# Spreading the residual gates with rounded products: two rounded parts of each row in place of one plain fp32 row

## The chip, the cores and the metric

The kernel runs on one core of one Trainium2 chip. The metric is the device time of one execution in microseconds (us), the median of the runs shown; a lower time is better.

## What is computed

Four trunk layers update 512 latent tokens (and 256 context tokens) of 1024 channels. Layers 0 and 3 mix the tokens by latent attention, layer 1 by banded attention, layer 2 by long convolutions. What matters here is the frame around the mixers:

```python
for layer in range(4):
    mx = silu(c) @ w_mod[layer] + b_mod[layer]          # latent stream
    mc = silu(c_ctx) @ w_mod[layer] + b_mod[layer]      # context stream
    shift, scale, gate = split(mx), split(mc)           # 1024 each
    h = rmsnorm(x, g_pre[layer]) * (1 + scale) + shift
    y = mixer(h) @ w_out                                # the gated mixer output
    x = x + gate * rmsnorm(y, g_post[layer])
```

The residual gate is one row of 1024 numbers per stream and layer; each token's row of y is multiplied by it. In layer 3 only the latent tokens are needed.

## The kernel before

**Numbers in two parts.** Weights and activations are split into two rounded parts (fp32r), hi and lo: ScalarE copies hi (lines 230, 341, 612), and VectorE or Pool subtracts to get lo (lines 233, 342, 613). A product is then three rounded products, hi hi, hi lo and lo hi.

**Tiles of w_out.** `w_out_phase` (line 591) goes through tiles of 128 tokens: 6 in layers 0 to 2, 4 in layer 3. In its order, the tile's share of the mixer output (`og`) is split into `o2` (lines 612 and 613; the first tile in two pieces, of 768 and 256 columns), 48 rounded products of 512 columns (line 621) make y in one of the two double PSUM banks, pb_69 and pb_70, and `post` (line 558) takes it from there: ScalarE's square with a sum (line 563), two small Pool operations for the power -1/2 (lines 358 and 359), VectorE's scaling into the same bank (line 565) and the addition to the residual (line 566). The bank is free for the tile after next when line 566 has read it. In layers 0 to 2 the norm of the next layer follows each tile.

**The gates.** `mod_g_unit` computes half a layer's gates at a time; the row block `m` (128x1024 fp32, an F slot) holds partial sums on some partitions and the bias on one. `gates_out` (line 484), called after the first tile's products, sums those rows and spreads them over all 128 partitions: a product with the 0/1 matrix `sel` (128x128 for each stream), 512 columns at a time (line 493), and multiplies the result by g_post (line 494). That is four plain fp32 products in each of layers 0 to 2 and two in layer 3; the records show each as two.

**What sets the order.** Each engine works through its own queue. The order in the queues is made by a scheduler that runs over the emitted program with its own model of times; what is emitted first isn't always first in a queue. Memory is set by the emission: two arenas, R for rounded and F for plain fp32 tiles, hand out slots. `slot` (line 88) takes, among the first free ones (three for R), the one that was freed longest ago. So one more request shifts which slot the following requests get, and with it what a tile has to wait for. In layer 2 the slots of a third memory, swing, change from plain to rounded when the layer's own work is done.

**Other lines that are named.** In layers 0 and 3 (latent attention) the last work before w_out is that of the heads: scores (line 872), maximum (876), exponential (879), reciprocal and scaling of the probabilities (880 and 881), their transposes (897, with copies in lines 341 and 342), the products with the values (911) and the gating into `og` (914). Line 441 is the modulation's products with w_mod; `setup_late` (line 394) loads constants, `sel` among them, while layer 0 is prepared; line 1376 splits values for the filters. Line 1562 is one of the last steps of layer 2's convolutions, line 1176 of layer 1's heads.

Of the kernel before, what the change touches and what calls it, by code (L numbers as in the profile page):

```python
# [12 lines left out]
F32 = mybir.dt.float32  # L13
# [6 lines left out]
P = 128  # L20
# [32 lines left out]
class Arena:  # L53
    """Words of SBUF tiles, handed out in emission order.

    Blocks of one kind of life are taken from the low end ("lo"); slots of a fixed size lie on a grid
    that starts at the high end, of which the first few that are free take turns."""
# [78 lines left out]
class Ring:  # L136
    """A few blocks that take turns"""
# [14 lines left out]
class Banks:  # L152
    """PSUM banks that take turns"""
# [9 lines left out]
class SubRing:  # L163
    """Parts of one slot that take turns"""
# [12 lines left out]
class Stream:  # L177
    """Chunks of weights in the order in which they are used: loaded and split ahead of their use"""
# [92 lines left out]
class Kern:  # L271
# [58 lines left out]
    def halves(self):  # L330
        """single banks of the double ones, the one in use last at the end"""
        pair = [self.ps_s[(self.is_ + 1) % 2], self.ps_s[self.is_ % 2]]
        return [x[:, c0:c0 + 512] for x in pair for c0 in (0, 512)]
# [10 lines left out]
    def gate2(self, out, ps):  # L344
        """2 silu(x) = x (1 + tanh(x / 2)); the values carry the half"""
# [9 lines left out]
    def rstd(self, ssq, n):  # L355
        """(ssq / n + eps) ** -0.5 on the Pool engine, in place"""
# [13 lines left out]
    def setup(self):  # L370
# [18 lines left out]
        for nm, key, shape in (("gkv", "a_g_kv_t", [P, 2, 2]), ("gq", "a_g_q_t", [P, 2, 4]), ("rope", "rope", [P, 4, 2, 64]),  # L389
                               ("sel", "sel", [P, 2, P]), ("sgn", "sgn", [P, 1]), ("cconv", "c_conv_t", [P, 24, 4])):  # L390
# [3 lines left out]
    def setup_late(self):  # L394
        """constants that the first filters and modulations do not need"""
        nc, io = self.nc, self.io
        for key, t in self.late.items():
            nc.sync.dma_start(out=t, in_=io[key])
        mf = self.fs(768)
# [18 lines left out]
    def plan_mod(self, layers):  # L418
        """units of modulation in the order in which they are done"""
# [13 lines left out]
    def mod_chunk(self, L, c, ps):  # L433
        """[128, 512] of this chunk: rows 32 j + s hold partial sums of stream s"""
# [12 lines left out]
    def mod_ab_unit(self, L, c, bank=None):  # L447
        """shift (c = 0, 1) and scale (c = 2, 3) of layer L as columns"""
# [22 lines left out]
    def mod_g_unit(self, L, c, bank=None):  # L471
        """half c of layer L's gates: a row for each stream's partial sums, one for the bias"""
# [10 lines left out]
    def gates_out(self, L):  # L483
        """gates times g_post, the same on every partition, for each stream"""
# [3 lines left out]
        for s, o in enumerate(g):  # L488
            nc.sync.dma_start(out=o.ap, in_=io["g_post"][L:L + 1].to_broadcast([P, D]))
            for c in range(2):  # L490
                cs = slice(512 * c, 512 * c + 512)
                ps = self.a()
                nc.tensor.matmul(ps, self.sel[:, s, :], m.ap[:, cs], start=True, stop=True)
                nc.vector.tensor_tensor(o.ap[:, cs], ps, o.ap[:, cs], op=ALU.mult)
        m.free()
        return g

# [1299 lines left out]
```

## Time and profile before

| what | value |
|---|---|
| median of 3 runs | 1951.24 us (1950.47 to 1952.38) |
| span of the profiled execution | 1949.5 us |
| that execution's own time | no figure beside the span is given |
| TensorE (PE) busy | 1835.7 us, 94% |
| VectorE (DVE) busy | 1189.3 us, 61% |
| ScalarE (ACT) busy | 811.7 us, 42% |
| Pool busy | 523.2 us, 27% |
| records of the gate products, line 493 | 28, from 550.5 to 1904.7 us |

How to read it: busy times are sums over the span. A row of the timeline gives the start, the length, the engine, the line, the operation, output and inputs with their shapes, how many follow each other in the row, and, in brackets, how long the engine was idle before and what ended that. Records of products overlap, so the step between two is shorter than the length of one.

### The profile page before, as it was taken

Reading aid. Unit: us, or ns where it says so; the run is one execution under the profiler, and the core shown is the slowest. Engines: PE = TensorE matmul, PEld = TensorE weight load, DVE = VectorE, ACT = ScalarE, POOL = GpSimd, SP = SyncE. Lnnn points to the kernel's source line nnn. Section 1 sums busy time; section 2 is a strip of 40 time slices with the busy share of each in tenths; the row PEclk is TensorE's granted clock in tenths of the full one; section 3 lists DMA queues with packets and bytes.
Section 4 is the critical chain, followed back from the end, with each engine's and each line's share of the span. In section 5 each row is a group of like instructions: output and inputs, shape, how many; then the busy total and the mean of one; then the engine's idle time right before and its main releaser. Section 6 shows DMA issues by size and latency. Waiting matters only on the chain. (4 is left out here: it accounts for less than half of the span.)

```text
span 1949.5 us, 29536 instructions
## 1 busy us (share of the span) xinstructions
PE 1835.7 (94%) x11244; PEld 1571.5 (81%) x11244; DVE 1189.3 (61%) x2364; ACT 811.7 (42%) x1686; POOL 523.2 (27%) x523
## 2 busy tenths in 40 slices
PE   5989999999999899999999899999998999999998
PEld 3557588999988888888858699999997787889986
DVE  6684234777755377677764445666668554477663
ACT  3472232545544255565653422222222343354451
POOL 5561000000213321222231344444444221000120
PEclk9989999999999999999999999999999999999999
DMA  6956521011133112222363622222221335310121
GB/s 216 269 163 205 179 79 31 23 33 34 52 110 110 55 57 74 77 74 67 98 217 108 201 71 72 70 76 76 76 77 58 123 112 152 96 33 23 44 76 54
DMA packets 161777, 186.27 MB, mean 96 GB/s; under 512 B 16600, under 2 KB 115800, under 8 KB 161636
## 3 DMA queue, kind: packets, MB, share of 16 engines
q1 hardware_dynamic: 161636, 184.39, 30.5%
q8 instruction: 88, 1.44, 0.3%
q14 instruction: 53, 0.43, 0.1%
HBM read 160.24 MB, written 24.12 MB: 95 GB/s over the span
## 5 line engine op out<-in xcount | busy, mean ns | idle before, releaser
L587 PE MATMUL pb<-arena_r 128*128 128x512 f32 (+1 forms) x1536 | 293.3, 345 | 8.6 <-DVE arena_f L1497 2.7
L587 PEld LDWEIGHTS pb<-arena_r 128*128 128x128 f32 x1536 | 239.3, 192 | 41.6 <-issue 6.3
L341 ACT ACTIVATE arena_r<-pa 128x384 fp32r<-128x384 f32 (+2 forms) x382 | 174.8, 478 | 207.0 <-PE pa L897 68.1
L342 DVE TENSOR_TENSOR arena_r<-pa,arena_r 128x384 fp32r<-128x384 f32 (+2 forms) x382 | 199.5, 537 | 92.3 <-ACT arena_r L341 90.2
L587 PE MATMUL pa<-arena_r,swing_R 128*128 128x512 f32 (+1 forms) x816 | 165.6, 355 | 0.6 <-DVE arena_r L342 0.4
L587 PEld LDWEIGHTS pa<-arena_r,swing_R 128*128 128x128 f32 x816 | 132.4, 188 | 21.8 <-DVE arena_r L342 0.6
L872 PE MATMUL pb<-arena_r 128*128 128x384 f32 (+1 forms) x720 | 141.4, 337 | 3.0 <-ACT arena_r L341 1.8
L233 POOL TENSOR_TENSOR swing_R<-arena_f,swing_R 128x1024 fp32r<-128x1024 f32 (+1 forms) x33 | 76.9, 2334 | 201.3 <-ACT swing_R L230 156.1
L872 PEld LDWEIGHTS pb<-arena_r 128*128 128x128 f32 x720 | 119.0, 189 | 5.1 <-ACT arena_r L341 2.5
L667 POOL TENSOR_TENSOR arena_f<-arena_f 128x128 f32<-128x128 f32 (+1 forms) x44 | 21.2, 482 | 364.0 <-DVE small L880 178.5
L621 PE MATMUL pb<-arena_r 128*128 128x512 f32 x480 | 115.2, 393 | 0.0
L358 POOL TENSOR_SCALAR small<-small 128x1 f32<-128x1 f32 x68 | 17.8, 261 | 350.9 <-ACT trash L563 133.5
L233 POOL TENSOR_TENSOR arena_r<-swing_F,arena_r 128x1024 fp32r<-128x1024 f32 x34 | 85.3, 2511 | 77.1 <-ACT arena_r L230 75.3
L621 PEld LDWEIGHTS pb<-arena_r 128*128 128x128 f32 x480 | 89.5, 188 | 20.4 <-issue 1.6
L911 PE MATMUL pa<-arena_r 128*128 128x256 f32 x624 | 91.4, 287 | 2.1 <-DVE arena_r L342 2.1
L911 PEld LDWEIGHTS pa<-arena_r 128*128 128x128 f32 x624 | 81.7, 190 | 4.7 <-ACT arena_r L341 2.5
L1067 PE MATMUL pa<-swing_R,arena_r 128*128 128x256 f32 x576 | 77.6, 285 | 4.7 <-DVE arena_f L348 3.5
L441 PE MATMUL pa<-arena_f,cst 128*32 128x512 f32 x372 | 71.5, 602 | 10.5 <-DMA arena_f<-in_w_mod_dram 9.7
L876 DVE TENSOR_REDUCE small<-pb 128x1 f32<-128x768 f32 (+1 forms) x80 | 67.5, 846 | 21.6 <-PE pb L872 20.7
L879 ACT ACTIVATE arena_f<-pb,small 128x768 f32<-128x768 f32 (+1 forms) x80 | 65.2, 816 | 33.7 <-DVE small L877 27.3
L1067 PEld LDWEIGHTS pa<-swing_R,arena_r 128*128 128x128 f32 x576 | 71.2, 189 | 6.6 <-DVE arena_f L348 4.9
L1048 PE MATMUL pa<-arena_r,swing_R 128*128 128x512 f32 (+1 forms) x384 | 73.7, 342 | 2.7 <-DVE arena_r L1074 1.1
(266 smaller groups left out, 4211.8 us busy)
## 6 DMA issues: line engine op xcount, KB each, us to landing
arena_f<-in_w_mod_dram SPq DMA_DIRECT2D x93, 512.0 KB
swing_F<-in_c_w_in_dram SPq DMA_DIRECT2D x31, 512.0 KB
kd<-arena_f SPq DMA_DIRECT2D x48, 256.0 KB
arena_f<-in_a_w_in_dram SPq DMA_DIRECT2D x24, 512.0 KB
arena_f<-kd SPq DMA_DIRECT2D x16, 768.0 KB
arena_f<-in_b_w_in_dram SPq DMA_DIRECT2D x20, 512.0 KB
x<-arena_f SPq DMA_DIRECT2D x18, 512.0 KB
arena_f<-in_a_w_out_dram SPq DMA_DIRECT2D x16, 512.0 KB
```

The source lines that it names most:

```text
L233: eng.tensor_tensor(lo, view, hi.bitcast(F32), op=ALU.subtract)
L341: self.nc.scalar.activation(hi, src, AF.Copy)
L342: self.nc.vector.tensor_tensor(lo, src, hi.bitcast(F32), op=ALU.subtract)
L441: nc.tensor.matmul(ps[32 * j:32 * j + 32, :], self.cst[:, k, :], w[:, k2, :], start=(k < 4), stop=(k >= 4), skip_group_check=True)
L587: nc.tensor.matmul(out, l, rhs(part, k, i), start=(k == 0 and q == 0), stop=(k == kt - 1 and q == 2))
L621: nc.tensor.matmul(ys[:, 512 * hf:512 * hf + 512], ov[:, part, k], wt[:, 0, 512 * hf:512 * hf + 512], start=(k == 0 and q == 0), stop=(k = ...
L872: nc.tensor.matmul(S[:, 512 * b:512 * b + w], l, r[:, k0 + w * b:k0 + w * b + w], start=(q == 0), stop=(q == 4))
L876: nc.vector.tensor_reduce(mx, Sv, axis=AX.XY, op=ALU.max)
L879: nc.scalar.activation(pr.v(nb, w), Sv, AF.Exp, bias=mx, scale=sc, accum_out=sm)
L911: nc.tensor.matmul(o[:, 0:256], vv[:, a_, kt % 3, P * hh:P * hh + P], ptv[i // nh][:, b_, i % nh], start=(i == 0 and q == 0), stop=(i == n ...
L1048: nc.tensor.matmul(o, l[:, k], self.h_at(h, part, k, t0, n), start=(k == 0 and i == 0), stop=(k == KD - 1 and i == 2))
L1067: nc.tensor.matmul(ps[:, 0:256], self.h_at(h, part, k, P * t, P), w, start=(k == 0 and i == 0), stop=(k == KD - 1 and i == 2))
```

## The change

`sel` becomes an fp32r tile: it is loaded into an F slot and cast by Pool. After the layer's gates are complete and before the first tile's `o2` is requested, the new `gates_split` requests an R slot, copies the gate rows into its hi part on ScalarE (line 509 of the new file), subtracts the lo part on Pool (line 510) and frees the F slot. `gates_out` then makes two rounded products into one bank, hi and lo, in place of one plain product. The 0/1 matrix is exact in either form. Lines of the new file are 5 to 17 higher: 493 is 499, 494 is 500, 563 is 579, 565 is 581, 566 is 582, 612 is 629, 613 is 630, 621 is 638, 872 is 889, 879 is 896, 881 is 898, 897 is 914, 911 is 928 and 914 is 931.

```diff
-                               ("sel", "sel", [P, 2, P]), ("sgn", "sgn", [P, 1]), ("cconv", "c_conv_t", [P, 24, 4])):
+                               ("sgn", "sgn", [P, 1]), ("cconv", "c_conv_t", [P, 24, 4])):
...
     def setup_late(self):
...
         for key, t in self.late.items():
             nc.sync.dma_start(out=t, in_=io[key])
+        self.sel = self.pool.tile([P, 2, P], F32R, name="sel")
+        sf = self.fs(256)
+        nc.sync.dma_start(out=sf.v(2, P), in_=io["sel"])
+        nc.gpsimd.tensor_copy(self.sel, sf.v(2, P))
+        sf.free()
...
     def gates_out(self, L):
...
                 ps = self.a()
-                nc.tensor.matmul(ps, self.sel[:, s, :], m.ap[:, cs], start=True, stop=True)
+                for part in range(2):
+                    nc.tensor.matmul(ps, self.sel[:, s, :], m.v(2, D)[:, part, cs], start=(part == 0), stop=(part == 1))
                 nc.vector.tensor_tensor(o.ap[:, cs], ps, o.ap[:, cs], op=ALU.mult)
...
+    def gates_split(self, L):
+        nc = self.nc
+        m, blk = self.mg[L], self.rs(2 * D)
+        v = blk.v(2, D)
+        nc.scalar.activation(v[:, 0], m.ap, AF.Copy)
+        nc.gpsimd.tensor_tensor(v[:, 1], m.ap, v[:, 0].bitcast(F32), op=ALU.subtract)
+        m.free()
+        self.mg[L] = blk
...
         self.fill_to("g", L)
+        self.gates_split(L)
         self.turns_f = 6
         self.M.cap_d = self.M.look_d = 0
         xts = [self.load_x(L, order[0])]
```

Three places show what this does to the queues. In the rows, pa_65 to pa_68 are single PSUM banks, pb_69 and pb_70 the double ones, arena_r and arena_f slots of the two arenas; a number at the end counts equal instructions in a row.

TensorE in layer 3, from the last head's products with the values to the third tile of w_out, before:

```order
L621 MATMUL pb_70<-arena_r 128x512 x4
L911 MATMUL pa_67<-arena_r 128x256 x8
L493 MATMUL pa_65<-arena_f,sel 128x512
L621 MATMUL pb_70<-arena_r 128x512 x8
L911 MATMUL pa_67<-arena_r 128x256
L621 MATMUL pb_69<-arena_r 128x512 x6
L621 MATMUL pb_69<-swing_R,arena_r 128x512 x3
L911 MATMUL pa_67<-arena_r 128x256 x8
L621 MATMUL pb_69<-swing_R,arena_r 128x512 x15
L621 MATMUL pb_69<-arena_r 128x512 x24
L621 MATMUL pb_70<-arena_r 128x512 x6
L621 MATMUL pb_70<-swing_R,arena_r 128x512 x18
```

And now:

```order
L638 MATMUL pb_69<-arena_r 128x512 x2
L638 MATMUL pb_69<-swing_R,arena_r 128x512 x15
L928 MATMUL pa_67<-arena_r 128x256 x8
L638 MATMUL pb_69<-swing_R,arena_r 128x512 x3
L638 MATMUL pb_69<-arena_r 128x512 x20
L638 MATMUL pb_70<-arena_r 128x512 x4
L638 MATMUL pb_69<-arena_r 128x512
L638 MATMUL pb_70<-arena_r 128x512 x2
L638 MATMUL pb_70<-swing_R,arena_r 128x512 x18
L638 MATMUL pb_70<-arena_r 128x512 x24
L638 MATMUL pb_69<-arena_r 128x512 x3
L638 MATMUL pb_70<-arena_r 128x512 x6
```

Before, the first tile (pb_70) is done in the midst of the last heads, and ends ahead of the second (pb_69). Now the second tile begins; behind 44 of its products come four of the first, one more of the second and the first's other 44. The second tile's last three products stand at the end, directly ahead of the third tile (pb_70).

VectorE's last rows in layer 3, before:

```order
L565 SCALAR_TENSOR_TENSOR pb_70<-pb_70,small,arena_f 128x1024
L914 TENSOR_TENSOR arena_f<-pa_67,arena_f 128x256
L566 TENSOR_TENSOR arena_f<-arena_f,pb_70 128x1024
L613 TENSOR_TENSOR arena_r<-arena_f,arena_r 128x1024 x2
L565 SCALAR_TENSOR_TENSOR pb_69<-pb_69,small,arena_f 128x1024
L566 TENSOR_TENSOR arena_f<-arena_f,pb_69 128x1024
L565 SCALAR_TENSOR_TENSOR pb_70<-pb_70,small,arena_f 128x1024
L566 TENSOR_TENSOR arena_f<-arena_f,pb_70 128x1024
```

And now:

```order
L931 TENSOR_TENSOR arena_f<-pa_67,arena_f 128x256
L630 TENSOR_TENSOR arena_r<-arena_f,arena_r 128x768
L630 TENSOR_TENSOR arena_r<-arena_f,arena_r 128x1024 x2
L581 SCALAR_TENSOR_TENSOR pb_70<-pb_70,small,arena_f 128x1024
L581 SCALAR_TENSOR_TENSOR pb_69<-pb_69,small,arena_f 128x1024
L582 TENSOR_TENSOR arena_f<-arena_f,pb_70 128x1024
L582 TENSOR_TENSOR arena_f<-arena_f,pb_69 128x1024
L581 SCALAR_TENSOR_TENSOR pb_70<-pb_70,small,arena_f 128x1024
L582 TENSOR_TENSOR arena_f<-arena_f,pb_70 128x1024
```

Before, each bank's scaling (565) is followed by its addition (566), and the first bank's pair stands ahead of the second's. Now the scaling of pb_69 (581) stands between the scaling and the addition of pb_70.

ScalarE at the end of layer 2, where the first tile's split in swing_R starts, before:

```order
L230 ACTIVATE arena_r<-arena_f 128x1024
L1564 ACTIVATE swing_F<-pa_68 128x256
L1565 ACTIVATE swing_F<-pa_65 128x128
L230 ACTIVATE arena_r<-arena_f 128x1024
L612 ACTIVATE swing_R<-arena_f 128x768
L612 ACTIVATE swing_R<-arena_f 128x256
L612 ACTIVATE swing_R<-arena_f 128x1024
```

And now:

```order
L230 ACTIVATE arena_r<-arena_f 128x1024
L1581 ACTIVATE swing_F<-pa_68 128x256
L1582 ACTIVATE swing_F<-pa_65 128x128
L230 ACTIVATE arena_r<-arena_f 128x1024
L509 ACTIVATE swing_R<-arena_f 128x1024
L629 ACTIVATE swing_R<-arena_f 128x768
L230 ACTIVATE arena_r<-arena_f 128x1024
L629 ACTIVATE swing_R<-arena_f 128x256
L629 ACTIVATE swing_R<-arena_f 128x1024
```

The new copy (line 509) stands behind the last copy of a weight (line 230) and ahead of the first tile's 768 columns, and one copy of a weight has moved ahead of its other 256 columns.

## The prediction

> **What bounds the kernel now.** I read the engine totals of the page first, then the group of the products that the change replaces, then the timeline of TensorE around them, and last the timelines of the other engines at the four places where w_out starts.
>
> ```profile
> span 1949.5 us, 29536 instructions
> PE 1835.7 (94%) x11244; PEld 1571.5 (81%) x11244; DVE 1189.3 (61%) x2364; ACT 811.7 (42%) x1686; POOL 523.2 (27%) x523
> L493 PE MATMUL pa<-arena_f,sel x28: 590/592/1062, 550.5 to 1904.7; 128*128 128x512 f32 x28
> ```
>
> TensorE is busy for 94% of the span, so a product that is made shorter can pay, but only where TensorE then goes straight on. The plain fp32 products of line 493 stand as 28 records, two for each of 14 products (layers 0, 1 and 2 have four each, layer 3 has two). Their width in the records overlaps, so their price is the step from one to the next.
>
> ```profile
> 1021.11 2.74 PE L493 MATMUL pa<-arena_f,sel 128*128 128x512 f32 x6
> 1910.25 21.20 PE pb L621 x93
> ```
>
> Six in a row take 2.74 us, the last of them 0.59, so the step is (2.74 - 0.59)/5 = 0.43 us. The second row, from the chain of waits, has 93 rounded products of the same shape (line 621): 21.20/93 = 0.228 us each. The profiled execution's span is 1949.5 us and its own time isn't given beyond that; the median of the three runs is 1951.24, so I make the sum on the span and carry its difference, 1.7 us, along unchanged.
>
> **The products themselves.** A product now costs 2 x 0.43 = 0.86 us, and will cost 2 x 0.228 = 0.46. Each of the 28 records saves 0.2 us: 5.6 us at most, 1.6 in each of layers 0 to 2 and 0.8 in layer 3. That is 0.29% of the time; about 0.2%, 3.9 us, is what a measurement of this kernel can tell from no change. So anything that costs 2 us at a w_out start decides.
>
> **The new steps.** gates_split adds in each layer one ScalarE copy and one Pool subtract of 128x1024, ahead of the first tile's o2.
>
> ```profile
> 1519.35 1.05 ACT L230 ACTIVATE arena_r<-arena_f 128x1024 fp32r<-128x1024 f32 x1
> 1520.29 2.09 ACT L612 ACTIVATE swing_R<-arena_f 128x768 fp32r<-128x768 f32 x3
> 1521.18 22.99 PE L621 MATMUL pb<-arena_r,swing_R 128*128 128x512 f32 x96
> 1515.99 1.91 PE L493 MATMUL pa<-arena_f,sel 128*128 128x512 f32 x2
> 1517.69 1.45 PE L1562 MATMUL pa<-arena_f,swing_F 128*128 128x128 f32 x8
> 1518.97 2.24 PE L493 MATMUL pa<-arena_f,sel 128*128 128x512 f32 x4
> 1883.55 2.70 DVE L881 TENSOR_SCALAR arena_f<-arena_f,small 128x768 f32<-128x768 f32 x1
> 1883.45 5.04 POOL L233 TENSOR_TENSOR arena_r<-arena_f,arena_r 128x1024 fp32r<-128x1024 f32 x2 [3.15 <-ACT arena_r L230]
> 1890.15 0.60 DVE L881 TENSOR_SCALAR arena_f<-arena_f,small 128x768 f32<-128x768 f32 x1
> ```
>
> The copy is 1.05 us by the row of line 230, the subtract 5.04/2 = 2.5 us by line 233. The cast of sel, 128x256, falls on Pool before the first subtract of line 1376, where Pool is idle:
>
> ```profile
> 27.69 2.52 POOL L1376 TENSOR_TENSOR swing_R<-arena_f,swing_R 128x512 fp32r<-128x512 f32 x2 [7.73 <-ACT swing_R L1374]
> ```
>
> The 7.73 us of idle time cover it; without that cover it would cost half of one such subtract, about 0.6 us. I take nothing.
>
> **Layer 2.** The copy stands in ScalarE's queue between the last L230 and the 768 columns of line 612 on which the first products wait. Both write the swing memory that the layer's last filter step holds until then. Against ScalarE's 1.05 us stands about 0.3: two gate products no longer lie at 1515.99, ahead of line 1562's at 1517.69, so that last step ends a little sooner. The first w_out product comes at some 1521.9 instead of 1521.18, 0.75 later. There the old gate products ran while TensorE waited for ScalarE anyway (the four at 1518.97), so removing them saves nothing, and four second parts, which wait for Pool's subtract, come after 48 products of the first tile: 4 x 0.228 = 0.9 us that was free before. Sum 0.75 + 0.9 = +1.7 us; bounds 0 and 2.6 (the whole copy and a second wait for Pool's 2.5 us in part).
>
> **Layers 0 and 1.**
>
> ```profile
> 550.98 2.19 PE L621 MATMUL pb<-swing_R,arena_r 128*128 128x512 f32 x7
> 553.13 1.02 PE L493 MATMUL pa<-arena_f,sel 128*128 128x512 f32 x2
> 553.58 1.16 PE L911 MATMUL pa<-arena_r 128*128 128x256 f32 x5
> 1008.64 1.12 PE L493 MATMUL pa<-arena_f,sel 128*128 128x512 f32 x2
> 1009.21 1.49 PE L621 MATMUL pb<-swing_R,arena_r 128*128 128x512 f32 x4
> ```
>
> In layer 0 the gate products stand amid others with no idle time, and the order of tiles on TensorE stays what it was: the whole 1.6 us is saved (bounds -1.6 and +1). In layer 1 the second tile's first products now stand before the first tile's, because the first tile's o2 has moved to a slot that comes free only after the last head; the first w_out product then waits for a copy of 1024 columns, 1.05 us, which stands behind the last head's gating: about 1010.3 instead of 1009.21. That and a tighter hand-over of the first bank take back the 1.6 us: I take 0 (bounds -1.6 and +2).
>
> **Layer 3, where I expect the most.** The block for the two gate parts takes the slot that the first tile's o2 had. That tile's o2 now lies where the last head's transposed probabilities are, and is filled only when they have been read. TensorE loses its filler:
>
> ```profile
> 1891.33 0.62 DVE L881 TENSOR_SCALAR arena_f<-arena_f,small 128x768 f32<-128x768 f32 x1
> 1894.35 0.49 ACT L341 ACTIVATE arena_r<-pa 128x384 fp32r<-128x384 f32 x1 [3.48 <-issue]
> 1894.87 0.56 DVE L342 TENSOR_TENSOR arena_r<-pa,arena_r 128x384 fp32r<-128x384 f32 x1 [2.92 <-ACT arena_r L341]
> 1900.68 0.42 DVE L914 TENSOR_TENSOR arena_f<-pa,arena_f 128x256 f32<-128x256 f32 x1 [3.56 <-PE pa L911]
> 1889.15 1.64 PE L621 MATMUL pb<-arena_r 128*128 128x512 f32 x6
> 1890.62 2.72 PE L621 MATMUL pb<-swing_R,arena_r 128*128 128x512 f32 x11
> 1896.87 1.55 PE L621 MATMUL pb<-arena_r 128*128 128x512 f32 x6
> 1913.58 6.99 PE L621 MATMUL pb<-arena_r 128*128 128x512 f32 x30
> ```
>
> Before, 17 products of the first tile at 1889.15, and more later, fill the waits of the last heads. After, those waits stand empty, and the second tile's products come first. They need this chain: the last scaling ends at 1891.95; six transposes (0.5), a split copy and subtract of them (0.49 + 0.56), nine products of line 911 (0.12 each, 1.1), the gating of line 914 (0.42), the split copy of 1024 columns (1.05), and some 0.6 for six hand-overs: 1896.65, an estimate. Then 96 products of w_out and 9 of the last head are still to do: 1896.65 + 21.9 + 1.1 = 1919.6. Before, the second tile ends with the 24th of the 30 at 1913.58, at 1919.05. So the lost filler costs about 0.5 us net, the saved 0.8 of the gate products counted in.
>
> The larger step is behind it. In the new order TensorE does all but three products of the second tile (pb_69), then those of the first (pb_70), and the three at the very end. VectorE's queue has the two post-norm halves crossed: L581 of pb_70, L581 of pb_69, then L582 of pb_70. The third tile's products write pb_70, so they wait for L582 of pb_70, which stands behind L581 of pb_69, which needs the sum of squares of a tile whose last product has just ended. The price of this chain is that of the same steps in the trace:
>
> ```profile
> 1919.30 1.02 ACT L563 ACTIVATE trash<-pb 128x1024 bf16<-128x1024 f32 x1 [6.46 <-PE pb L621]
> 1920.22 0.19 ACT L563 ACTIVATION_READ_ACCUMULATOR trash<-pb 128x1 f32 x1
> 1920.50 0.19 POOL L358 TENSOR_SCALAR small<-small 128x1 f32<-128x1 f32 x1 [11.35 <-ACT trash L563]
> 1920.78 0.55 POOL L359 TENSOR_TENSOR small<-small,mhalf 128x1 f32<-128x1 f32 x1
> 1921.36 1.29 DVE L565 SCALAR_TENSOR_TENSOR pb<-pb,small,arena_f 128x1024 f32<-128x1024 f32 x1 [7.07 <-POOL small L359]
> 1922.69 1.22 DVE L566 TENSOR_TENSOR arena_f<-arena_f,pb 128x1024 f32<-128x1024 f32 x1
> 1935.63 5.63 PE L621 MATMUL pb<-arena_r 128*128 128x512 f32 x24
> 1944.73 1.22 DVE L566 TENSOR_TENSOR arena_f<-arena_f,pb 128x1024 f32<-128x1024 f32 x1
> ```
>
> From the start of a square to the end of line 566 is 1923.91 - 1919.30 = 4.6 us. Here it starts some 0.8 us late, since ScalarE squares pb_70 first (its products end 3 x 0.228 us earlier, the square takes 1.2): 1919.6 + 0.8 + 4.6 = 1925.0, some 5.4 us in which TensorE stands idle. Before it had no wait there, since the other bank's 48 products (11 us) covered the same chain. From 1925.0 go the last two tiles, 96 x 0.228 = 21.9, and what follows the last product in the trace, 1949.5 - (1935.63 + 5.63) = 8.2: 1955.1 to 1955.3. Layer 3 is +5.7 us. Bounds: +1.5 (were the chain half covered) and +8 (with the rival of the blocked VectorE below).
>
> **Start of the program.** The late load of sel through an F slot moves a few transposes, projections and weight loads around; no row prices that. The nearest is the wait for modulation weights, and it could go either way by a few of its pieces:
>
> ```profile
> L441 PE MATMUL pa<-arena_f,cst 128*32 128x512 f32 x372 | 71.5, 602 | 10.5 <-DMA arena_f<-in_w_mod_dram 9.7
> ```
>
> I take 0, bounds -3 and +3.
>
> **Sum.** -1.6 + 0 + 1.7 + 5.7 + 0 = +5.8 us: span 1955.3, time 1951.24 + 5.8 = 1957.0.
>
> **Rivals.**
>
> *The blocked VectorE (+1 to +3, slower still).* In the rows above, the scaling of 128x768 (line 881) takes 0.60 us at 1890.15 and 2.70 at 1883.55, where it begins 0.1 us after a Pool subtract begins, and it ends about when the first of that pair does. In layer 3 the new subtract follows Pool's last L233, which ends at 1883.45 + 5.04 = 1888.5, and so lies at 1888.5 to 1891.0, over the last two scalings: the first would end near 1891.3 in place of 1890.75, and the last, by the queue, about 1 us after its 1891.95. With as much in layer 0: 1958 to 1960, point 1958.8. [...] It decides if a scaling falls inside L510's 2.4 us.
>
> *The saving carries through (faster).* TensorE is the bound, and if the chain at pb_70 is covered, 5.6 us come off: 1945.6. For it speak the 94%; against it the order of VectorE's queue, in which nothing can run past L581 of pb_69. It decides if the three last pb_69 products run 5 us earlier than the order shows, or if the start wins several of the 9.7 us that TensorE waits there for weights.
>
> *Only the filler is lost (no change).* If the crossed halves cost nothing, the sum is 5.8 - 5.4 = +0.4: 1951.6. It holds if the wait for pb_70 is taken at L581 and not at L582, or if the other layers save more than I count.
>
> **How the numbers follow.** Forecast (1957.0) 0.47; blocked VectorE 0.26; only the filler lost 0.13; saving carried 0.14. Slower is the first two, less a little for the start's bound: 0.72; the same 0.14; faster 0.14. The range leaves out the carried saving and a little above: from 1950.0, which takes in the case without change with 1.6 us to spare, to 1960.5, the forecast with the blocked VectorE and part of the start's bound.
>
> **What would show it.** In the profile after: the group of line 499 with 28 records at about half the step; TensorE idle some 5 us, released by VectorE's L582, before the third tile of layer 3; no products of line 638 before about 1896 on the new span's scale, and L898 of over 2 us beside L510. The forecast is wrong if TensorE has no idle time over 2 us between the second and third tile of layer 3, or if the order there leaves L582 of pb_70 early; and if the stretch up to the first w_out differs by over 3 us, the start has decided.

## The result, and the profile after

The changed kernel takes 1974.4 us (median of 4 runs, 1973.51 to 1975.4), the kernel before 1951.01 us (4 runs, 1950.47 to 1952.38): the ratio is 1.0116, with a 95% interval of 1.0099 to 1.0134. It is slower, as forecast, but by 23 us and not by 6; the forecast's range ended at 1960.5. One of the eight runs of a variant told below took 3003 us at a mean granted clock (the share of its full clock that TensorE was given) of 0.56, and is left out of its ratio and median.

The head of the page after, and the groups that answer to those of before (busy time, mean ns of one, idle time ahead of them and what ended it; the spreading products stand in two groups, by the memory that they read):

```profile
span 1973.6 us, 29538 instructions
PE 1839.7 (93%) x11244; PEld 1575.8 (80%) x11244; DVE 1185.7 (60%) x2364; ACT 816.8 (41%) x1690; POOL 534.4 (27%) x528
L499 PE MATMUL pa<-arena_r,sel 128*128 128x512 f32 x20 | 5.9, 398 | 0.0
L499 PE MATMUL pa<-swing_R,sel 128*128 128x512 f32 x8 | 2.4, 422 | 2.3 <-ACT swing_R L509 2.3
L638 PE MATMUL pb<-arena_r 128*128 128x512 f32 x480 | 115.4, 395 | 5.2 <-DVE arena_f L582 5.2
L446 PE MATMUL pa<-arena_f,cst 128*32 128x512 f32 x372 | 74.0, 622 | 13.9 <-DMA arena_f<-in_w_mod_dram 13.7
```

The w_out products of line 638 have an idle time that was 0.0 before (line 621 there), and the wait for modulation weights has grown from 9.7 to 13.7 us:

```profile
L621 PE MATMUL pb<-arena_r 128*128 128x512 f32 x480 | 115.2, 393 | 0.0
```

To see where the time went, I cut the span at the same instructions in each trace (the first and last scores of layers 0 and 3, the first and last w_out product of a layer) and compared the lengths. The kernel before was profiled three times and the changed one twice, since single executions differ:

| stretch | before: 1st, 2nd, 3rd profile | after: 1st, 2nd | difference of the means |
|---|---|---|---|
| start, up to layer 0's first scores | 337.9, 334.4, 336.4 | 342.0, 339.8 | +4.6 |
| layer 0's heads (first to last scores) | 197.2, 197.2, 197.3 | 196.2, 196.6 | -0.9 |
| layer 0's w_out (last scores to last w_out product) | 78.3, 78.4, 78.4 | 76.7, 76.8 | -1.6 |
| layer 1 with its w_out | 470.1, 470.0, 475.2 | 475.7, 478.4 | +5.3 |
| layer 2 up to w_out | 437.6, 437.5, 435.3 | 439.5, 437.7 | +1.8 |
| layer 2's w_out | 72.9, 72.9, 72.9 | 77.8, 75.5 | +3.7 |
| layer 3 up to its last scores | 290.4, 290.4, 289.5 | 289.5, 290.3 | -0.2 |
| layer 3's last scores to last w_out product | 56.8, 56.6, 56.7 | 68.1, 65.9 | +10.3 |
| tail | 8.2, 8.2, 8.2 | 8.2, 8.2 | 0 |

The w_out stretches of layers 0, 2 and 3 of before agree within 0.2 us; the start and layer 1 of one and the same program differ by 3.5 and 5.2 us. That will matter for what can be said of them.

**Layer 3.** The timeline of TensorE from the first w_out product on, and of VectorE at the wait:

```profile
1911.92 1.07 PE L638 MATMUL pb<-arena_r 128*128 128x512 f32 x4
...
1928.93 6.30 PE L638 MATMUL pb<-arena_r 128*128 128x512 f32 x27
1940.40 2.90 PE L638 MATMUL pb<-arena_r 128*128 128x512 f32 x6 [5.17 <-DVE arena_f L582]
1943.10 5.81 PE L638 MATMUL pb<-swing_R,arena_r 128*128 128x512 f32 x18
```

```profile
1936.65 2.48 DVE L581 SCALAR_TENSOR_TENSOR pb<-pb,small,arena_f 128x1024 f32<-128x1024 f32 x2 [14.34 <-POOL small L359]
1939.04 2.34 DVE L582 TENSOR_TENSOR arena_f<-arena_f,pb 128x1024 f32<-128x1024 f32 x2
```

Both scalings run ahead of the addition for which TensorE waits, 5.17 us. But then six products take 2.90 us, where the row of the 27 just ahead has 0.228 each. The stretches of this trace with the granted clock (the number after the five busy times; the last two columns are the DMA engines' share and GB/s):

```profile
1935.00:1940.00 5.00, 0.24 (x2) 0.00 (x0) 3.35 (x3) 1.82 (x4) 1.47 (x4) 0.95 0.00 0
1940.00:1943.00 3.00, 2.60 (x6) 2.15 (x7) 1.39 (x2) 0.00 (x0) 0.00 (x0) 0.50 0.64 258
1943.00:1948.00 5.00, 5.00 (x16) 3.91 (x16) 0.00 (x0) 0.00 (x0) 0.00 (x0) 0.67 0.14 55
1948.00:1952.00 4.00, 4.00 (x19) 3.26 (x19) 0.00 (x0) 0.00 (x0) 0.00 (x0) 1.00 0.00 0
1939.50:1946.20 6.70, 5.80 (x14) 4.57 (x15) 1.89 (x2) 0.00 (x0) 0.00 (x0) 0.50 0.39 157
1946.40:1952.00 5.60, 5.60 (x26) 4.58 (x25) 0.00 (x0) 0.00 (x0) 0.00 (x0) 1.00 0.00 0
```

The clock is at 0.50 from 1939.5 to 1946.3 and then at 1.00 again; the 0.67 is the mean over a stretch that holds both. So TensorE works at half its clock for 5.9 us after the wait (1940.4 to 1946.3), which can cost half of that, an estimate of 3.0 us. Before, the clock was 1.00 in all of this (in each of the stretches from 1889.15 to 1941.26). That is a second price of the wait.

**Layer 2.** The end of the convolutions and the first tile, with VectorE and Pool beside it:

```profile
1517.40 0.51 PE L1574 MATMUL pa<-arena_r 128*128 128x256 f32 x2 [2.87 <-ACT arena_r L1559]
1518.51 0.97 PE L1574 MATMUL pa<-arena_r 128*128 128x256 f32 x6 [0.61 <-DVE arena_r L1560]
1521.29 3.78 PE L1574 MATMUL pa<-arena_r 128*128 128x256 f32 x16 [1.80 <-DVE arena_r L1560]
1524.87 1.81 PE L1579 MATMUL pa<-arena_f,swing_F 128*128 128x128 f32 x8
1528.93 1.31 PE L499 MATMUL pa<-swing_R,sel 128*128 128x512 f32 x4 [2.26 <-ACT swing_R L509]
1530.04 1.91 PE L638 MATMUL pb<-arena_r,swing_R 128*128 128x512 f32 x4
1532.75 12.31 PE L638 MATMUL pb<-arena_r,swing_R 128*128 128x512 f32 x44 [0.80 <-DVE swing_R L630]
1544.90 1.09 PE L499 MATMUL pa<-swing_R,sel 128*128 128x512 f32 x4
```

```profile
1528.96 2.92 POOL L510 TENSOR_TENSOR swing_R<-arena_f,swing_R 128x1024 fp32r<-128x1024 f32 x1 [4.12 <-ACT swing_R L509]
```

```profile
1529.70 2.99 DVE L630 TENSOR_TENSOR swing_R<-arena_f,swing_R 128x768 fp32r<-128x768 f32 x1
```

The old gate products no longer lie in these waits: the wait ahead of 1517.40 is 2.87 us, and of the products behind it the last 16 take 3.78 us. The same row of before reads 2.61:

```profile
1513.58 2.61 PE L1557 MATMUL pa<-arena_r 128*128 128x256 f32 x16 [1.79 <-DVE arena_r L1543]
```

That difference need not be the change's: in the first profile of a variant that keeps the old gate products (the slot alone, below) the same 16 products take 3.78 us too.

```profile
1522.55 3.78 PE L1559 MATMUL pa<-arena_r 128*128 128x256 f32 x16 [1.81 <-DVE arena_r L1545]
```

What is new is the clock at the start of w_out. These are the first microseconds of w_out in the first profile of before and in the two profiles of the change:

```profile
1521.18:1531.00 9.82, 9.77 (x42) 7.59 (x42) 5.68 (x7) 2.89 (x4) 1.84 (x1) 1.00 0.82 299
1530.04:1536.60 6.56, 5.76 (x14) 4.06 (x13) 5.26 (x4) 1.77 (x3) 1.84 (x1) 0.50 0.94 350
1529.16:1531.24 2.08, 1.91 (x5) 0.99 (x3) 2.08 (x2) 1.26 (x3) 1.32 (x1) 0.50 0.88 333
```

The clock is 1.00 again from 1536.7 in the first profile of the change and from 1531.3 in the second. So 6.6 and 2.1 us of w_out lie at half the clock, which by the same estimate can cost 3.3 and 1.1 of the 4.9 and 2.6 us by which it is longer. The remaining 1.6 and 1.5 us hold the second parts (0.9) and the waits for VectorE's line 630.

And VectorE's subtract for the first 768 columns takes 2.99 us beside Pool's new one, and TensorE waits 0.80 us for it (0.28 in the second profile).

**Layer 1.** In both profiles of the change TensorE has three waits around the start of w_out that before doesn't have, 3.0 us together (these rows are of the first):

```profile
1014.34 0.86 PE L1193 MATMUL pa<-arena_r 128*128 128x256 f32 x4 [1.41 <-DVE arena_f L1199]
1015.96 1.19 PE L638 MATMUL pb<-swing_R,arena_r 128*128 128x512 f32 x4 [0.75 <-ACT arena_r L629]
1041.46 4.44 PE L638 MATMUL pb<-swing_R,arena_r 128*128 128x512 f32 x18 [0.79 <-DVE arena_f L582]
```

**The start.** One wait for modulation weights, before and after:

```profile
208.18 2.54 PE L441 MATMUL pa<-arena_f,cst 128*32 128x512 f32 x16 [1.51 <-DMA arena_f<-in_w_mod_dram]
```

```profile
209.91 3.64 PE L446 MATMUL pa<-arena_f,cst 128*32 128x512 f32 x16 [6.64 <-DMA arena_f<-in_w_mod_dram]
```

5.1 us more of waiting, and 16 products that take 1.1 us longer behind it.

**The products themselves** got as much cheaper as forecast: four parts in a row take 1.09 us, the last 0.39, a step of (1.09 - 0.39)/3 = 0.23 us.

### The profile page after: what moved, and what is told of

It is laid out like the page before. It is cut to its first block, busy times and chain, and to the rows that moved or that the text cites. A ratio compares the mean times of both kernels' runs of the same rounds, so it can differ in the third digit from the quotient of the medians.

```text
span 1973.6 us, 29538 instructions
## 1 busy us (share of the span) xinstructions
PE 1839.7 (93%) x11244; PEld 1575.8 (80%) x11244; DVE 1185.7 (60%) x2364; ACT 816.8 (41%) x1690; POOL 534.4 (27%) x528
## 5 line engine op out<-in xcount | busy, mean ns | idle before, releaser
L603 PE MATMUL pa<-arena_r,swing_R 128*128 128x512 f32 (+1 forms) x816 | 165.7, 354 | 0.6 <-DVE arena_r L342 0.4
L603 PEld LDWEIGHTS pa<-arena_r,swing_R 128*128 128x128 f32 x816 | 132.2, 188 | 21.9 <-DVE arena_r L342 0.6
L446 PE MATMUL pa<-arena_f,cst 128*32 128x512 f32 x372 | 74.0, 622 | 13.9 <-DMA arena_f<-in_w_mod_dram 13.7
L230 ACT ACTIVATE arena_r<-swing_F 128x1024 fp32r<-128x1024 f32 x34 | 36.0, 1063 | 100.7 <-PE pb L603 90.9
```

What stands on the lines that cost most here:

```text
L230: nc.scalar.activation(hi, view, AF.Copy)
L446: nc.tensor.matmul(ps[32 * j:32 * j + 32, :], self.cst[:, k, :], w[:, k2, :], start=(k < 4), stop=(k >= 4), skip_group_check=True)
L603: nc.tensor.matmul(out, l, rhs(part, k, i), start=(k == 0 and q == 0), stop=(k == kt - 1 and q == 2))
```

## The experiments

Each is told with its edit and the ratio of its time to that of the kernel before on the same chip, with a 95% interval. The slot alone and the staging alone are edits of the kernel before, all others of the changed one. "Start" and the like are the stretches of the table, against the first profile of before. A line of waits gives the total in us, how many there were, and the longest.

### The slot alone

```diff
+        self.gslot = self.rs(2 * D)     # in w_out_phase, where the split would stand
...
+        self.gslot.free()               # at the end of gates_out
```

> The kernel before, with one thing of the change: at the place of the split an R slot is requested, left unused, and freed after the gates have been spread. No copy, no subtract, no rounded gate product, sel as before. Slot theory (the slot alone moves the tiles of w_out): the stretch from layer 3's last scores to the end of its w_out grows by 7 to 10 us (idle TensorE before the third tile 5 us, the slower clock after it 2.8, the lost filler 0.5 to 2), layer 1's start of w_out by 0 to 3; in all 1959 to 1964 us. Rival (the added work costs the time: copies, subtracts, second parts): within 2 us of before, 1949 to 1953.

Measured: ratio 1.0063 (1.0042 to 1.0084), median 1963.3 us beside 1952.7. Layer 3's last stretch is 9.4 us longer in this profile and in a second one, without a single copy or rounded gate product. TensorE's waits in it, and its clock behind them:

```profile
PE pb L623 <- DVE arena_f L567: 4.9, 1, 4.9
```

```profile
1936.00:1941.00 5.00, 5.00 (x12) 3.94 (x13) 0.89 (x1) 0.00 (x0) 0.00 (x0) 0.50 0.52 210
```

Layers 0 and 2's w_out are unchanged within 0.1 us. Layer 1 with its w_out is 7.5 us longer (6.6 in the second profile). The slot theory holds: the request alone, with nothing in the slot, moves the tiles, and the ratio of 1.0063 is about half of the loss of 1.0116.

### The split requested late

```diff
-        self.gates_split(L)             # ahead of the first tile's o2
...
             if n == 0:
+                self.gates_split(L)     # behind the first tile's products
                 g = self.gates_out(L)
```

> The changed kernel with the split requested behind the first tile's o2 and products, right ahead of the spreading; all the new work is kept. Slot theory: the first tile of layer 3 is first again, no idle TensorE over 2 us before its third tile, and that layer's w_out loses the 11 us that it gained; layers 1 and 2 lose part of theirs; the start's 3 to 4 us stay: 1955 to 1962 us. Rival (added work): the same copies and subtracts are still made, so at most 5 us come off: 1969 to 1975.

Measured: ratio 1.0062 (1.0039 to 1.0084). Layer 3's last stretch is 0.45 us shorter than before, with all of the new work in it, and TensorE's longest wait there is another, of 1.1 us:

```profile
PE pa L914 <- DVE arena_f L898: 1.1, 1, 1.1
```

Layer 0's w_out keeps its gain (-1.7 us), layer 1's w_out gains 0.9; layer 2's keeps its loss (+4.7). The median, 1965, lies above the 1955 to 1962 that I expected. The profile doesn't show why: its execution took 1956.9 us, as expected, and the six other runs 1962.6 to 1966.7.

### The staging of sel: alone, and taken out

```diff
-                               ("sel", "sel", [P, 2, P]), ("sgn", "sgn", [P, 1]), ("cconv", "c_conv_t", [P, 24, 4])):
+                               ("sgn", "sgn", [P, 1]), ("cconv", "c_conv_t", [P, 24, 4])):
...
+        self.sel = self.pool.tile([P, 2, P], F32, name="sel")
+        sf = self.fs(256)
+        nc.sync.dma_start(out=sf.v(2, P), in_=io["sel"])
+        nc.gpsimd.tensor_copy(self.sel, sf.v(2, P))
+        sf.free()
```

> The kernel before, with only the loading of sel changed: through an F slot and a Pool copy into an fp32 tile; the gate products stay plain fp32. Theory that the staging of sel makes the start longer: the stretch up to layer 0's first scores grows by 3 to 5 us and the time is 1954 to 1956. Rival (the start's 4 us come from elsewhere, for instance from how the scheduler places later work): under 1 us in the start, 1950 to 1952.

And the changed kernel without it, with sel loaded into its own fp32 tile and a second, rounded tile cast from that:

```diff
+        self.selr = self.pool.tile([P, 2, P], F32R, name="selr")
+        nc.gpsimd.tensor_copy(self.selr, self.sel)
...
+                    nc.tensor.matmul(ps, self.selr[:, s, :], m.v(2, D)[:, part, cs], start=(part == 0), stop=(part == 1))
```

> The changed kernel with sel loaded as before into its fp32 tile and cast from there by Pool, with no F slot taken for it; all else as in the change. If the staging through the slot makes the start longer: the start is within 1 us of before and the time 1969 to 1972, layer 3's loss of 11 us unchanged. If not: the start keeps 3 to 4 us, 1973 to 1976.

Measured: the staging alone gives 1.0031 (1.0018 to 1.0045), 6 us; the change without it 1.0080 (1.0054 to 1.0105), 7 us less than the change. TensorE's waits for modulation weights up to 342 us, with the staging alone and in the change without it:

```profile
PE pa L446 <- DMA arena_f<-in_w_mod_dram: 13.1, 7, 6.5
```

```profile
PE pa L443 <- DMA arena_f<-in_w_mod_dram: 7.5, 7, 1.9
```

Before it was 6.1 in all and 1.9 at the longest. Over all traces, the eight profiles of kernels with the staging have a start 1.6 to 9.0 us longer than the first profile of before (mean 4.2), the ten without it (before's three among them) -4.3 to +2.3 (mean -0.8): by the means the staging costs 5 us. (In single profiles it went past what I expected: +9.0 and +4.5 us with the staging alone, -4.3 in the change without it.) Pool's cast, which I had looked at, is not what costs: the change without the staging makes it too. A slot more in the F arena changed the turn of the slots behind it, and with it the order in which loads are issued. That order is the same with the staging alone as in the change, and in the change without the staging it is that of before, up to the end of the start. Issued by SyncE's sequencer (SPq) around the long wait, before and after:

```profile
200.05 4.55 SPq L211 DMA_DIRECT2D arena_f<-in_w_mod_dram  x3
206.04 0.37 SPq L211 DMA_DIRECT2D arena_f<-in_a_w_in_dram  x1
```

```profile
201.54 0.37 SPq L211 DMA_DIRECT2D arena_f<-in_w_mod_dram  x1
203.25 0.37 SPq L211 DMA_DIRECT2D arena_f<-in_a_w_in_dram  x1
203.66 11.33 SPq L211 DMA_DIRECT2D arena_f<-in_w_mod_dram  x4
```

Before, the load of `a_w_in` stood behind these loads of w_mod; now loads of w_mod stand behind it.

### Where TensorE stands idle, other work

```diff
             if last and n == 1:
+                ps = self.a()
+                for i in range(20):
+                    nc.tensor.matmul(ps, ov[:, i % 2, i % KD], ws[i % KD][1][0][:, 0, 0:512], start=(i == 0), stop=(i == 19))
```

> The changed kernel with 20 products more in layer 3, whose result nobody reads, put on TensorE between the second tile's last products and the third tile, where it stood idle for 5.2 us: 20 x 0.228 = 4.6 us of work. Clock theory (the idle time lowers the granted clock, 0.50 and 0.67 in the 8 us behind it, and that costs 2.8 us more): the clock stays at 1.00 there and the stretch of the third and fourth tile gets 2 to 3 us shorter than with the change, though TensorE does more. Rival (the slow first products have another cause, such as operands that come late): the stretch stays as long or grows.

Measured: from the end of the second tile's last product to the end of the fourth tile it is 5.4 us more than before, where the change had 8.1 (second profile 7.5): 2.1 to 2.7 us less, with 20 products more. The third tile's first products and the clock:

```profile
1936.92 1.60 PE L638 MATMUL pb<-arena_r 128*128 128x512 f32 x6 [0.57 <-DVE arena_f L582]
```

```profile
1936.00:1941.00 5.00, 4.43 (x20) 3.36 (x19) 1.91 (x2) 0.00 (x0) 0.00 (x0) 1.00 0.52 210
```

Six products take 1.60 us and not 2.90, the clock is 1.00. So the slower clock behind the idle TensorE cost 2.1 to 2.7 us here, about half of the wait again. (The whole kernel is at 1.0106, 1.0080 to 1.0132: too little changes to show there.)

### Layer 2 with the old products kept beside the new

```diff
+        if L == 2:                      # in gates_split, requested late, sel not staged
+            for s in range(2):
+                for c in range(2):
+                    nc.tensor.matmul(self.a(), self.sel[:, s, :], m.ap[:, 512 * c:512 * c + 512], start=True, stop=True)
```

> The split requested late as in the run above, sel kept in its fp32 tile and cast from there, and in layer 2 the four old plain gate products kept as well, their result unread. Clock theory for layer 2: with them the waits at the end of the convolutions are filled as before, the 16 products of line 1574's copy take 2.6 us in place of 3.8, and the end of layer 2 up to the last w_out product loses 2 to 4 of the 4.7 us. Rival (the 4.7 us are the new copy, the subtract and the second parts themselves): it loses under 1 us.

Measured: 0.9993 (0.9978 to 1.0007). Layer 2 with its w_out is 3.4 us longer than before, against 4.4 with the late split alone. The products at the end of the convolutions are as slow as without, but w_out itself begins at the full clock:

```profile
1513.46 5.06 PE L1579 MATMUL pa<-arena_r 128*128 128x256 f32 x22 [2.43 <-DVE arena_r L1565]
1518.33 1.07 PE L511 MATMUL pa<-arena_f,sel 128*128 128x512 f32 x2
1522.13:1532.00 9.87, 9.87 (x43) 7.91 (x43) 6.19 (x5) 4.79 (x6) 2.42 (x1) 1.00 0.66 243
```

5.06 us for 22 is 0.23 each, as 3.78 for 16. By layer 2 as a whole 1 us came back, and by its w_out alone 1.7 (3.0 over before, where the late split had 4.7): neither the 2 to 4 of the theory nor, in w_out, the under 1 of its rival.

All 18 profiles together say more than this one. Up to w_out, layer 2 takes 435.5 to 439.5 us in the eight in which it is split and 435.3 to 440.0 in the ten others, with a mean of 437.4 in both: what differs there belongs to the execution. Its w_out takes 72.9 us in each of the ten others and 75.4 to 77.8 in the eight. In the ten, and in this variant, w_out lies at a clock of 1.00 from its first product on; in the seven with the split and without the old products 1.8 to 6.6 us of its first 7 lie at 0.50. Less half of that time, it is 1.5 to 1.6 us longer in all five profiles that split early, and 2.1 to 3.3 in the three that split late, where hi and lo parts (8 x 0.23 = 1.8 us) both stand inside it. So the loss of the change in layer 2 is about 1.6 us for second parts and waits, and by that estimate 1.1 to 3.3 us for the clock.

### The lo part on VectorE

```diff
-        nc.gpsimd.tensor_tensor(v[:, 1], m.ap, v[:, 0].bitcast(F32), op=ALU.subtract)
+        nc.vector.tensor_tensor(v[:, 1], m.ap, v[:, 0].bitcast(F32), op=ALU.subtract)
```

> The changed kernel with the lo part subtracted by VectorE in place of Pool; the slot is requested as early as in the change. Blocked-VectorE theory: the first 768 columns of layer 2 are no longer slowed (2.99 us against some 0.9), so layer 2's w_out loses 2 to 3.5 of its 4.9 us; in layer 3 the two last scalings are not slowed by the new subtract and the first w_out product comes 1 to 2.4 us earlier, while the 5.2 us of idle time before the third tile stay: 3 to 6 us under the change. Rival (Pool's subtract only runs beside): both w_out stretches stay within 0.5 us, or grow by VectorE's own 1.2 us.

Measured: 1.0110 (1.0090 to 1.0131): not the 3 to 6 us under the change that I expected. The place itself did change. VectorE in layer 2:

```profile
1531.19 1.22 DVE L510 TENSOR_TENSOR swing_R<-arena_f,swing_R 128x1024 fp32r<-128x1024 f32 x1
1532.33 0.95 DVE L630 TENSOR_TENSOR swing_R<-arena_f,swing_R 128x768 fp32r<-128x768 f32 x1
```

0.95 us in place of 2.99, so beside Pool's subtract it had been held up for 2 us. But layer 2's w_out is 2.9 us over before, within what the change's two profiles show (4.9 and 2.6): the wait of 0.3 to 0.8 us that it ended was all that it cost. In layer 3 the first two tiles end 2.0 to 3.6 us earlier than with the change; the 5.2 us of waiting stay, as expected. The theory is right on the held-up subtract and wrong on the gain.

With the late split in addition (both edits together):

> The changed kernel with both mends: the split requested late and its lo part on VectorE; sel through its slot, layer 2 split too. Slot and blocked-VectorE theories together: layer 3's w_out within 0.5 us of before, layer 2's at 1 to 2.5 us over before (second parts 0.9, the slower clock after the longer waits), layer 0's 1.6 under: 2 to 4 us under the late split alone. Rival (layer 2's loss is all clock and second parts): layer 2 keeps 4 us or more.

Measured: 1.0037 (1.0020 to 1.0054); layer 3's last stretch 0.9 us under before, layer 0's w_out 1.7 under, layer 2's 3.9 over. Layer 2 did not come down to the 1 to 2.5 us that I expected.

### The change in layers 0, 1 and 3 only

The split requested late, sel not staged, layer 2 plain; first with the lo part on Pool:

```diff
-        self.gates_split(L)
...
+                if L in (0, 1, 3):
+                    self.gates_split(L)
...
-                for part in range(2):
-                    nc.tensor.matmul(ps, self.sel[:, s, :], m.v(2, D)[:, part, cs], start=(part == 0), stop=(part == 1))
+                if L in (0, 1, 3):
+                    for part in range(2):
+                        nc.tensor.matmul(ps, self.selr[:, s, :], m.v(2, D)[:, part, cs], start=(part == 0), stop=(part == 1))
+                else:
+                    nc.tensor.matmul(ps, self.sel[:, s, :], m.ap[:, cs], start=True, stop=True)
```

> The change made only in layers 0, 1 and 3, with the split requested late and sel cast from its fp32 tile; layer 2 keeps the plain products. If the losses are those of the slot (layers 1 and 3) and of layer 2's end, none is left, and the saved products show: layer 0's w_out 1.6 us shorter, layer 3's 0.4, layer 1's 0 to 1: 2 to 3 us under the kernel before on the same chip. Rival (the start or layer 1's heads lose what is saved): within 1 us or slower.

Measured: 0.9989 (0.9974 to 1.0005), not told apart from no change; the 2 to 3 us that I expected don't show. By stretches: layer 0's w_out 1.6 us shorter, layer 1's 0.9, layer 3's last 0.2, layer 2's w_out equal. Then with the lo part on VectorE:

> The version that the runs point to: the split in layers 0, 1 and 3 only, requested late, its lo part on VectorE, sel cast from its fp32 tile, layer 2 plain. Theory (slot, idle TensorE with its slower clock, and blocked VectorE were the losses): layer 0's w_out 1.6 us under before, layer 1 with its w_out 0 to 1 under, layer 3's heads and w_out within 0.5 of before or up to 1 under; in all 2 to 4 us under the kernel before. Rival (layer 1's 5 us belong to the split itself): layer 1 is 3 us or more over before and the time the same or slower.

Measured: 0.9966 (0.9952 to 0.9979): median 1948.4 us beside 1953.9 of the kernel before on that chip. This version beats both kernels. Its profile shows 1.6 us less in layer 0's w_out, 1.0 in layer 1's and 0.8 in layer 3's last stretch, 3.4 in all; layer 1's heads were 3.4 us longer in this one execution, so the rest of the 5.5 us is not placed by it.

### The same programs again

> The kernel before, unchanged, for a second profile of it: how much do its stretches differ from one execution to another? If the 4 to 5 us that all variants show in layer 1 and the shifts of up to 9 us at the start belong to the edits, every stretch agrees with the first profile within 1 us. If they are what executions differ by, the start and layer 1 differ here too, by 2 to 8 us, while the four w_out stretches agree within 0.5 us.

> The changed kernel, unchanged, for a second profile of it. If layer 1's 5.3 us and the four w_out stretches (layer 2: 4.9, layer 3: 11.3 us longer) belong to the program, they come again within 0.5 us, and only the start differs. If layer 1's 5.3 us come from how Pool and VectorE happen to meet in one execution, they differ by over 2 us.

Layer 1 (without its w_out) was 395.6 in the second profile of before, like the first, and 5.3 to 7.0 us longer with the change: the program, it seemed. Since nearly all variants had 5 us there, also the one that touches only sel, four more profiles followed:

> The kernel before, unchanged, a third profile. If layer 1's stretch belongs to the program, it is again within 1 us of 395.7 us; if it differs from execution to execution by the meeting of Pool and VectorE, it may lie up to 5 us above.

> The kernel with only the staging of sel changed, a second profile. Program theory: layer 1 is 5 us longer again, though the order of its products is that of before (only the order of weight loads differs there). Execution theory: it is anywhere between 0 and 5.

> The split in layers 0, 1 and 3, requested late, lo on Pool: a second profile. Program theory: layer 1 is within 1 us of before again. Execution theory: anywhere between 0 and 5 above.

> The kernel before with only the unused slot, a second profile. Up to layer 1's last heads its order is that of before. Program theory: layer 1 with its w_out is 7.5 us longer again. Execution theory: it differs from that by over 2 us. Layer 3's w_out is 9 us longer again by either.

Measured, against the first profile of before: the kernel before +5.0 us in its third profile; the staging alone +5.2 in the first and -0.1 in the second; the late split without layer 2 0.0 and +5.0; the slot alone +9.6 and +8.7 (its w_out -2.1 both times). So the 5 us belong to the execution for the most part. What the slot adds shows when layer 1 and its w_out are taken together: 475.5 to 478.4 us in the seven profiles of kernels that request it early, 469.2 to 475.3 in the eleven others, means 477.2 and 472.4.

## Why the prediction was right in its sign and wrong in its size

Of the 17 us that the forecast lacks, 4.6 lie in the start, 5.3 in layer 1, 3.8 in layer 2 and 4.6 in layer 3 (less 1.1 us in layer 0's heads and ahead of layer 3's last scores). The steps that failed are the two terms that were put at nothing, the start and layer 1, and the waits, which were priced by their length alone, without the clock behind them.

**Layer 0 (-1.6 us): right.** -1.6 in each profile; the step of the rounded products was 0.23 as put down.

**Layer 3 (+5.7, measured +10.3): the mechanism right, the size wrong.** The order's promise came true to the row: the wait for L582 of pb_70 was 5.17 us against 5.4 forecast. Two terms were missed. The step "From 1925.0 go the last two tiles, 96 x 0.228 = 21.9" took the full clock for granted; the two tiles took from 1940.4 to 1965.4 (the span less the tail of 8.2), 25.0 us, and 24.4 in the second profile, where before took 22.2: 2.8 and 2.2 us for the clock. A slower clock in the middle of the kernel stood in the profile of before too, around the gate products at the end of layer 2, and I used the durations of those rows without asking why they were longer: two gate products take 1.91 us at 1515.99, at a clock of 0.50, and two take 1.12 us at 1008.64, at 1.00. The stretch of before (the 0.77 is its mean, 0.50 up to 1518.5 and 1.00 behind it):

```profile
1516.15:1521.18 5.03, 4.91 (x16) 2.29 (x14) 3.65 (x8) 2.39 (x5) 0.98 (x2) 0.77 0.60 200
```

What a wait of 5 us does to the clock, none of the rows that I had quoted shows; in the profile of the change the 0.50 set in during the wait of 5.17 us and lasted for 5.9 us of work behind it. The rows of layer 2 were ground enough to allow for a second price of the wait, and the sum has none.

The other miss is the lost filler, forecast at 0.5 us net: the second tile ends 37.9 us after the last scores (36.3 in the second profile), where before it was 34.8, so 3.2 and 1.6 us were lost. The first tile starts at 1911.92, where the last scores of layer 3 ran 12.9 us later than before, so at 1899.1 on the old scale, against 1896.65 forecast; in the second profile it is 1897.4. Between the two profiles lies the clock again, which in the first stood at 0.50 from 1905.4 to 1908.6.

**The blocked VectorE: seen in the times, a part of the lost filler.** Beside Pool's new subtract, the scaling took 1.79 us where 0.60 is its time:

```profile
1901.09 2.36 POOL L510 TENSOR_TENSOR arena_r<-arena_f,arena_r 128x1024 fp32r<-128x1024 f32 x1
```

```profile
1902.08 1.79 DVE L898 TENSOR_SCALAR arena_f<-arena_f,small 128x768 f32<-128x768 f32 x1
```

It ends 0.4 us after the subtract, about where that rival put it, though it is shorter than the 2 us that were to be its sign. With the lo part on VectorE the first tile starts 2.0 us earlier, counted from the last scores, than in the second profile of the change, though one such scaling still takes 1.81 us there, in a stretch in which Pool is busy for 4.34 of 5.01 us. Why an operation of VectorE gets longer beside one of Pool, no run shows. I had given this rival a chance of 0.26 and left it out of the sum, though the row of before (2.70 us) was one of a kind with it. Alone it would have given 1958.8, far from 1974.4 as well.

**Layer 2 (+1.7, measured +5.5 with what lies ahead of w_out).** The second parts came as forecast (0.9). The copy did not: from line 1562's last row to the first w_out product it is 5.17 us after (1524.87 to 1530.04), 5.14 in the second profile, and was 3.49 before (1517.69 to 1521.18), so 1.7 more and not 0.75, since the four hi parts (the row at 1528.93) stand there too. Over all profiles, though, the part ahead of w_out is no longer than without the split, and the +1.8 there is what executions differ by. In w_out the step that failed is "removing them saves nothing": it cost. With the old products in the waits just ahead, w_out ran at the full clock in eleven profiles out of eleven; without them part of its first 7 us lay at half the clock in seven out of seven, which by the estimate above cost 1.1 to 3.3 us in the change.

**Layer 1 (0, measured +5.3).** The swap of the first tiles happened, and so did the wait for the copy (0.75 us for L629). But two more waits came with it (1.41 and 0.79 us), and the 1.6 us saved do not cover the three, 3.0 us. By the means over 18 profiles 4.8 us go with the early slot; the rest of them is not placed.

**The start (0, bounds -3 and +3, measured +4.6).** The row that I quoted for it, the wait for modulation weights, was the right one: its longest single wait went from 1.9 us to 6.64. I bounded it by "a few of its pieces" and priced the changed order of the loads at nothing. By the prediction's own sign (a stretch up to the first w_out that differs by over 3 us; it was 3.7 by the means) the start had a say of its own.

Of the other rivals, "the saving carries through" fell with the wait, and "only the filler is lost" with it: TensorE waited for L582, as the order in VectorE's queue had said. The sign was right by the wait that was forecast, and not by luck alone; the total was 17 us off by the four places above.

## What to carry to other kernels

A new buffer from a shared pool is a change to the schedule of everything that asks after it: request it after the tiles on the critical path, and look at the order of the loads as well as that of the engines. The wait of 5.2 us on TensorE had a second price in the clock behind it, 2.8 and 2.2 us in the two profiles of the change; and products that look wasteful may be what fills such a wait: with 20 that nobody reads in it, the clock stayed at 1.00. The 0.2 us saved on each of 28 records, 5.6 us at most, were worth less than that one new wait with its second price, so find the waits first.

## What the runs showed that I had not expected

- The granted clock fell to 0.50 in the course of 5.2 us of idle time on TensorE or right behind it, and was 1.00 again 5.9 us after work began (4.5 in the second profile, 3.5 with the lo part on VectorE); with the same 5 us filled by products that nobody reads, it stayed at 1.00. So one and the same wait had a second price of 2.8, 2.2 and 1.6 us.
- One and the same program differs by execution in single stretches, not evenly: layer 1 without its w_out took 395.7, 395.6 and 400.8 us in three profiles of the kernel before, while the w_out stretches of layers 0, 2 and 3 agreed within 0.2 us. Differences of 5 us in one profile are to be read stretch by stretch, with a second profile.
- A VectorE subtract of 128x768 from SBUF took 2.99 us beside a Pool subtract of 128x1024 and 0.95 without.
